# Swapping two entries of a hand-written TensorE order: head 2's transposes ahead of head 3's scores

## The chip, the cores and the metric

The kernel runs on one core of a Trainium2 chip. The core has five engines with instruction streams of their own: TensorE (PE; its weight loads are shown apart as PEld), VectorE (DVE), ScalarE (ACT), GpSimd (POOL) and SyncE (SP, which here issues transfers). TensorE writes its results into PSUM, eight banks of 128 x 512 float32; VectorE and ScalarE move them from there into the on-chip memory SBUF. The metric is device time in microseconds (us), the median of several runs. Lower is better.

## The reference: what is computed

One layer of a causal decoder for 512 tokens of width 1024, in float32: a mixing sublayer (stick-breaking attention with 8 heads beside a short gated convolution), a cross-attention into 256 fixed memory tokens with 4 heads of width 256, a SwiGLU FFN with 2816 hidden channels, and a final RMS norm. The change touches the memory sublayer only:

```
q = (h @ w_q).reshape(b, s, MEM_HEADS, MEM_HEAD_DIM)
kv = (m @ w_kv).reshape(b, mlen, 2, MEM_HEADS, MEM_HEAD_DIM)
scores = jnp.einsum('bshd,bmhd->bhsm', q, k)
probs = jax.nn.softmax(scores / math.sqrt(MEM_HEAD_DIM), axis=-1)
o = jnp.einsum('bhsm,bmhd->bshd', probs, v)
x = x + o.reshape(b, s, D_MODEL) @ w_o
```

(casts to float32 and the RMS norms of `x` and `mem` are left out here).

## The kernel before, in words

Every float32 operand is split into a high and a low part of the type float32r (names that end in `h` and `l`): ScalarE casts the high part, VectorE subtracts it from the original to get the low part. A product is then three matmuls, high x high, high x low and low x high. This is `mm3` (L158 to L161), and `split` (L169) makes the pairs. Weights come through `load_w` (L143): a transfer on SP's queue, a cast `wh` (L154), a subtraction `wl` (L155).

The kernel goes through the sublayers one after another: projections and mixing, the merge, the output projection, the queries of the memory attention, the memory attention, the FFN, the final norm.

In the memory attention the work of a head h, numbered 0 to 3, is cut into parts:

- `mem_q(h)` splits the queries, on ScalarE and VectorE alone. `mem_k(m)` makes 128 rows of keys; a head has two.
- `mem_scores(h)` (L828): 24 matmuls of 256 columns into two PSUM tiles `sc`, then the softmax, still unturned: maxima `mx` (VectorE, L844), the scaled negative `nb` (L847), four exponentials with their sums (ScalarE, L854), a reciprocal `rsu` (L858), and four scalings of the weights `pr` (VectorE, L860).
- `mem_turn(h)` (L865): eight 128 x 128 transposes of `pr` on TensorE into two PSUM tiles `pt`, and their split into `pth` (ScalarE, L173) and `ptl` (VectorE, L174).
- `mem_v(n)` (L811): the values of two heads at once, 96 matmuls of 512 columns, split into `vmh` and `vml` (L176, L177). Heads 2 and 3 need `mem_v(1)`.
- `mem_out(h)` (L873): twice six matmuls of 512 columns (values by turned weights), each six into a PSUM tile `om` that is split into `omh` and `oml`.
- `last(m, k0, k1)` is the output projection's block m, k steps k0 to k1 (function `block`, L617). Two k steps belong to each head: 0 to 5 need the outputs of heads 0 to 2, steps 6 and 7 that of head 3. Its PSUM tile is called `r`.

TensorE's order is written by hand: a list of parts (L885 to L892) stands inside `tc.manual_schedule(engines={mybir.EngineType.PE})`, so TensorE executes its instructions in the order in which the list calls the parts. ScalarE's and VectorE's order in this stage is left to a planner, which runs when the kernel is built: it simulates the engines and takes, for each, among the instructions that it believes ready the one that stands first in the code. On the chip each engine then runs its own instructions in the planned order, and waits where an input is not there.

The tiles come from pools with a fixed number of buffers: `sc` and most `om` from the pool `z` (4 PSUM banks), `pt` and head 1's `om` from the pool `o` (2 banks), `vm` and the projection's first blocks from the pool `mm` (2 banks), split results from a pool of 50 SBUF units, `pr` from a pool of 7.

Of the kernel before, what the change touches and what calls it, by code (L numbers as in the profile page):

```python
# [44 lines left out]
def hybrid_layer(ctx: ExitStack, tc: tile.TileContext, xT_d, memT_d, cols_d, wv_d, win_d,  # L45
# [838 lines left out]
    with tc.manual_schedule(engines={mybir.EngineType.PE}):  # L884
        for part, *args in ((mem_q, 0), (mem_k, 0), (mem_k, 1), (mem_scale,), (mem_k, 2), (mem_k, 3),  # L885
                            (mem_q, 1), (mem_scores, 0), (mem_k, 4), (mem_k, 5), (mem_scores, 1),
                            (mem_q, 2), (mem_k, 6), (mem_k, 7), (mem_turn, 0), (mem_v, 0),
                            (mem_turn, 1), (mem_scores, 2), (mem_q, 3), (mem_out, 0), (mem_out, 1),
                            (mem_v, 1), (mem_scores, 3), (mem_turn, 2), (mem_out, 2),
                            (last, 0, 0, 6), (last, 1, 0, 2), (mem_turn, 3), (last, 1, 2, 6),  # L890
                            (mem_out, 3), (last, 2, 0, 6, otile), (last, 0, 6, 8), (last, 1, 6, 8),
                            (last, 2, 6, 8)):  # L892
            part(*args)
        for m in range(3, KD):
            last(m, 0, KD)
# [305 lines left out]
```

## Time and profile before

| | us |
|---|---|
| three runs | 857.15, 858.88, 859.0 (median 858.88) |
| profiled execution | 856.19 |
| its span, first to last instruction | 854.5 |
| TensorE busy | 843.9 |
| VectorE busy | 644.7 |
| ScalarE busy | 460.6 |

The granted TensorE clock was 0.999 of full speed. Of 114.71 MB moved, 110.65 MB were read from device memory, 132 GB/s over the span. The memory attention's stage, from the first scores to the end of head 3's output, lies between 398.4 and 469.6 us of the span.

In the rows of the profile, `L870 PE MATMUL pt<-ident,pr` means line 870, TensorE, a matmul into the tile `pt` from `ident` and `pr`. In a timeline the first column is the start in us from the span's start, the second the duration, `x8` the number of instructions merged in a row, and the brackets at the end give how long the engine sat idle before and what released it. In a list of waits the columns are us in total, times, and the longest.

### The profile page before, as it was taken

The numbers are of one execution on the slowest core, as the hardware profiler recorded it, in microseconds if no ns is written. First come the engines' busy times: TensorE is split into PE (matmuls) and PEld (weight loads), VectorE is DVE, ScalarE is ACT, GpSimd is POOL, SyncE is SP. The second block draws the span as 40 slices with busy tenths as digits, with TensorE's granted clock in tenths as the row PEclk, the third lists the DMA queues.
The fourth block names the chain that finished last, engine by engine and source line by source line (L and its number), as shares of the span: only waits on it lengthen the run. The fifth ranks groups of instructions, "written<-read, shape, count | busy, mean of one in ns | idle before, by whom it ended". The sixth has DMA issues, their size and how long they took to land.

```text
span 854.5 us, 13535 instructions
## 1 busy us (share of the span) xinstructions
PE 843.9 (99%) x5200; PEld 757.8 (89%) x5200; DVE 644.7 (75%) x1106; ACT 460.6 (54%) x822; POOL 76.9 (9%) x101
## 2 busy tenths in 40 slices
PE   9999999999999999999998999999999999999997
PEld 7888787888888888999987889999999999888997
DVE  8769889986454467878764789888888778876864
ACT  7556766664333345666563666555544556652444
POOL 1011112211000001000000110111111110010002
PEclk9999999999999999999999999999999999999999
DMA  8432232218323343664431428777677775462312
GB/s 297 130 117 82 92 106 81 86 50 276 111 94 99 99 119 91 181 200 151 147 102 49 128 57 198 187 182 186 174 180 188 190 189 168 130 148 65 104 37 100
DMA packets 47217, 114.71 MB, mean 134 GB/s; under 512 B 4912, under 2 KB 9008, under 8 KB 47152
## 3 DMA queue, kind: packets, MB, share of 16 engines
q1 hardware_dynamic: 38704, 97.82, 34.9%
q0 software_dynamic: 8160, 15.73, 11.5%
q8 instruction: 41, 0.67, 0.3%
q10 hardware_dynamic: 288, 0.29, 0.1%
q14 instruction: 24, 0.20, 0.1%
HBM read 110.65 MB, written 2.10 MB: 132 GB/s over the span
## 4 chain that ended last, share of the span: by engine, by line
PE 98%; DVE 1%; ACT 0%; issue 0%; POOL 0%; DVEq 0%; ACTq 0%; POOLq 0%
PE z L710 20%; PE y L710 10%; PE pr L159 8%; PE pr L160 8%; PE pr L161 8%; PE v L710 5%; PE r L159 3%; PE r L160 3%; PE r L161 3%; PE f L160 3%; PE f L159 3%; PE f L161 3%; PE v L265 3%; PE br L160 2%; PE br L159 2%; PE br L161 2%
## 5 line engine op out<-in xcount | busy, mean ns | idle before, releaser
L154 ACT CAST wh<-wr 128x1024 fp32r<-128x1024 f32 x90 | 94.2, 1050 | 131.5 <-issue 48.4
L155 DVE TENSOR_TENSOR wl<-wr,wh 128x1024 fp32r<-128x1024 f32 x90 | 109.7, 1222 | 18.0 <-ACT wh L154 17.4
L159 PE MATMUL pr<-xgh,wh 128*128 128x512 f32 x288 | 112.6, 391 | 0.0
L160 PE MATMUL pr<-xgl,wh 128*128 128x512 f32 x288 | 112.3, 390 | 0.0
L161 PE MATMUL pr<-xgh,wl 128*128 128x512 f32 x288 | 112.2, 390 | 0.0
L710 PE MATMUL z<-xdh,wf 128*128 128x256 f32 x480 | 95.7, 283 | 0.0
L710 PEld LDWEIGHTS z<-xdh,wf 128*128 128x128 f32 x480 | 78.9, 192 | 0.0
L710 PE MATMUL z<-xdl,wf 128*128 128x256 f32 x240 | 67.9, 283 | 0.0
L733 ACT COPY sa<-z 128x256 f32<-128x256 f32 x52 | 19.4, 373 | 85.5 <-PE z L710 85.5
L161 PEld LDWEIGHTS pr<-xgh,wl 128*128 128x128 f32 x288 | 54.1, 188 | 11.4
L159 PEld LDWEIGHTS pr<-xgh,wh 128*128 128x128 f32 x288 | 54.1, 188 | 11.2 <-DVE rv L128 0.3
L160 PEld LDWEIGHTS pr<-xgl,wh 128*128 128x128 f32 x288 | 54.1, 188 | 10.7
L701 DVE TENSOR_TENSOR wf<-s,wf 128x512 fp32r<-128x512 f32 x60 | 41.3, 690 | 22.7 <-ACT wf L700 21.5
L667 POOL DMA_DIRECT2D ws<-in_w_ffn_in_dram x22 | 26.5, 1202 | 305.3 <-DMA ws<-in_w_ffn_in_dram 147.3
L700 ACT CAST wf<-ws 128x512 fp32r<-128x512 f32 x60 | 36.9, 618 | 25.0 <-PE r L160 10.1
L160 PE MATMUL f<-actl,wh 128*128 128x512 f32 (+1 forms) x144 | 49.3, 342 | 0.0
L159 PE MATMUL f<-acth,wh 128*128 128x512 f32 (+1 forms) x144 | 49.3, 342 | 0.0
L161 PE MATMUL f<-acth,wl 128*128 128x512 f32 (+1 forms) x144 | 49.1, 342 | 0.0
L692 DVE TENSOR_TENSOR wf<-wg,wf 128x1024 fp32r<-128x1024 f32 x30 | 36.7, 1224 | 16.1 <-ACT wf L691 16.0
L710 PE MATMUL y<-xch,wf 128*128 128x256 f32 x240 | 48.5, 283 | 0.0
L710 PE MATMUL v<-xoh,wf 128*128 128x256 f32 x240 | 48.5, 283 | 0.0
L710 PE MATMUL z<-xf,wf 128*128 128x256 f32 x360 | 48.4, 283 | 0.0
(295 smaller groups left out, 2296.6 us busy)
## 6 DMA issues: line engine op xcount, KB each, us to landing
wr<-in_w_in_dram SPq DMA_DIRECT2D x36, 512.0 KB, 3.5
ws<-in_w_ffn_in_dram SPq DMA_DIRECT2D x22, 512.0 KB, 4.0
ws<-in_w_ffn_in_dram POOLq DMA_DIRECT2D x22, 512.0 KB, 5.8
wg<-in_w_ffn_in_dram SPq DMA_DIRECT2D x22, 512.0 KB, 4.6
wr<-in_w_ffn_out_dram SPq DMA_DIRECT2D x14, 512.0 KB, 3.5
a<-in_w_ffn_in_dram SPq DMA_DIRECT2D x22, 256.0 KB, 4.8
wr<-in_w_branch_dram SPq DMA_DIRECT2D x8, 512.0 KB, 3.5
wr<-in_w_mix_out_dram SPq DMA_DIRECT2D x8, 512.0 KB, 3.5
```

The costliest lines, as they stand in the source:

```text
L154: after(nc.scalar.copy(h2, raw), lead[-1:])
L155: lows.append(nc.vector.tensor_tensor(out=l2, in0=raw, in1=f(h2), op=ALU.subtract))
L159: nc.tensor.matmul(ps, a[0], b[0], start=start, stop=False, **kw)
L160: nc.tensor.matmul(ps, a[0], b[1], start=False, stop=False, **kw)
L161: nc.tensor.matmul(ps, a[1], b[0], start=False, stop=stop, **kw)
L265: nc.tensor.matmul(vps[t], xg[k][a][:, sl], wv[k][b], start=k == 0 and (a, b) == (0, 0), stop=k == KD - 1 and a == 1)
L667: nc.gpsimd.dma_start(s13, a[:, 0:4:3, :], accum_op=ALU.add)
L692: nc.vector.tensor_tensor(out=lo, in0=pair, in1=f(hi), op=ALU.subtract)
L700: nc.scalar.copy(hi, raw)
L701: nc.vector.tensor_tensor(out=lo, in0=raw, in1=f(hi), op=ALU.subtract)
L710: nc.tensor.matmul(ps[:, :HS], a, b, start=i < 3 and k == 0 and j == 0, stop=k == KP - 1 and j == 2, skip_group_check=True)
L733: nc.scalar.copy((s[:, :HS], None, None, s[:, HS:], t[:, :HS], t[:, :HS])[i], z)
```

## The change

Two neighbours of TensorE's list change places. Before, head 3's scores are written, then head 2's turn and head 2's output; after, head 2's turn is written first, then head 3's scores, then head 2's output. (The parts are numbered from 0: `mem_turn, 2` is the third head's turn, `mem_scores, 3` the fourth head's scores.)

```
-                            (mem_v, 1), (mem_scores, 3), (mem_turn, 2), (mem_out, 2),
+                            (mem_v, 1), (mem_turn, 2), (mem_scores, 3), (mem_out, 2),
                             (last, 0, 0, 6), (last, 1, 0, 2), (mem_turn, 3), (last, 1, 2, 6),
                             (mem_out, 3), (last, 2, 0, 6, otile), (last, 0, 6, 8), (last, 1, 6, 8),
                             (last, 2, 6, 8)):
```

Since the parts are called in this order, the ScalarE and VectorE instructions of head 2's turn (two casts `pth`, two subtractions `ptl`) also stand ahead of head 3's softmax in the code that the planner reads. Instructions, sizes, pools and transfers are the same.

More of the change, by code (lines that the diff above doesn't have):

```diff
@@ L888, in hybrid_layer @@
                             (mem_turn, 1), (mem_scores, 2), (mem_q, 3), (mem_out, 0), (mem_out, 1),
-                            (mem_v, 1), (mem_scores, 3), (mem_turn, 2), (mem_out, 2),
+                            (mem_v, 1), (mem_turn, 2), (mem_scores, 3), (mem_out, 2),
                             (last, 0, 0, 6), (last, 1, 0, 2), (mem_turn, 3), (last, 1, 2, 6),
```

## The prediction

> **What bounds the kernel now.** I read the page's busy shares and its chain first, to see whether one engine carries the span.
>
> ```profile
> PE 843.9 (99%) x5200; PEld 757.8 (89%) x5200; DVE 644.7 (75%) x1106; ACT 460.6 (54%) x822; POOL 76.9 (9%) x101
> PE 98%; DVE 1%; ACT 0%; issue 0%; POOL 0%; DVEq 0%; ACTq 0%; POOLq 0%
> ```
>
> TensorE is busy 99% and makes up 98% of the chain. What a change of order can win is therefore bounded by TensorE's waits, so the view of waits for TensorE alone over the whole span comes next (columns: us in total, times, longest).
>
> ```profile
> PE om L159 <- ACT pth L173: 2.5, 1, 2.5
> PE warm L224 <- DVE neg L91: 1.6, 1, 1.6
> PE om L160 <- DVE ptl L174: 0.5, 1, 0.5
> ```
>
> There are three, and two of them lie at the place of the change: head 2's output product `om` waits for the two halves of the transposed weights, `pth` (a ScalarE cast) and `ptl` (a VectorE subtraction). The timeline of TensorE shows the place (start, duration, and in brackets the idle time before):
>
> ```profile
> 447.33 0.39 PE L161 MATMUL vm<-wh,mgl 128*128 128x512 f32 x1
> 447.56 0.28 PE L159 MATMUL sc<-kmh,mqh 128*128 128x256 f32 x1
> ...
> 450.43 1.04 PE L870 MATMUL pt<-ident,pr 128*128 128x128 f32 x8
> 454.01 0.50 PE L159 MATMUL om<-pth,vmh 128*128 128x512 f32 x1 [2.54 <-ACT pth L173]
> 454.98 0.50 PE L160 MATMUL om<-ptl,vmh 128*128 128x512 f32 x1 [0.47 <-DVE ptl L174]
> ...
> 457.62 0.39 PE L159 MATMUL r<-omh,wh 128*128 128x512 f32 x1
> ...
> 460.56 0.39 PE L160 MATMUL r<-oml,wh 128*128 128x512 f32 x1
> ...
> 463.06 1.03 PE L870 MATMUL pt<-ident,pr 128*128 128x128 f32 x8
> ```
>
> The order is: head 3's scores (`sc`, 447.56), head 2's eight transposes (450.43), head 2's output (454.01), then the projection (`r`, 457.62), and at 463.06 head 3's own turn. Head 2's turn reads softmax results that were done by 436.25 (the scaling at 435.63, quoted below), so nothing makes it late but its place. Directly behind it stands the product that needs it. ScalarE and VectorE show why the wait is as long as 2.5 us:
>
> ```profile
> 448.34 1.04 ACT L154 CAST wh<-wr 128x1024 fp32r<-128x1024 f32 x1
> 451.18 0.57 ACT L854 ACTIVATE pr<-sc,nb,r1s 128x256 f32<-128x256 f32 x1 [1.80 <-DVE nb L847]
> ...
> 453.37 1.08 ACT L173 CAST pth<-pt 128x512 fp32r<-128x512 f32 x2
> ```
>
> ```profile
> 449.19 0.69 DVE L844 TENSOR_REDUCE mx<-sc 128x2 f32<-128x512 f32 x1
> 449.80 1.22 DVE L155 TENSOR_TENSOR wl<-wr,wh 128x1024 fp32r<-128x1024 f32 x1
> ...
> 453.71 0.62 DVE L860 TENSOR_SCALAR pr<-pr,rsu 128x256 f32<-128x256 f32 x2
> 454.24 1.28 DVE L174 TENSOR_TENSOR ptl<-pt,pth 128x512 fp32r<-128x512 f32 x2
> ```
>
> The transposes end at 450.43 + 1.04 = 451.47, but the four exponentials of head 3's softmax hold ScalarE from 451.18, and the casts `pth` follow only at 453.37. On VectorE `ptl` stands behind the scaling of head 3's weights. So head 3's whole softmax lies inside head 2's wait.
>
> **What the new order does, step by step.** The diff swaps two entries of the list by which TensorE's instructions are written out. No instruction is added or removed: eight transposes, 24 score matmuls and all the evictions stay. No DMA belongs to either entry, so the queues of SP and POOL are passed by nothing. ScalarE's and VectorE's orders are left to the planner, which goes by code order and readiness; the swap raises `pth` and `ptl` ahead of head 3's softmax in both.
>
> The new order already stands once in this kernel, one head earlier: `mem_v` 0, turn 1, scores 2, output 0. That stage is the price list, since the shapes are the same. TensorE, ScalarE and VectorE there:
>
> ```profile
> 427.46 1.03 PE L870 MATMUL pt<-ident,pr 128*128 128x128 f32 x8
> 428.25 0.36 PE L159 MATMUL sc<-kmh,mqh 128*128 128x256 f32 x1
> ...
> 431.21 0.40 PE L159 MATMUL om<-pth,vmh 128*128 128x512 f32 x1
> 431.44 0.40 PE L160 MATMUL om<-ptl,vmh 128*128 128x512 f32 x1
> ...
> 433.96 0.39 PE L159 MATMUL om<-pth,vmh 128*128 128x512 f32 x1
> ```
>
> ```profile
> 429.19 1.07 ACT L173 CAST pth<-pt 128x512 fp32r<-128x512 f32 x2
> ...
> 433.11 0.57 ACT L854 ACTIVATE pr<-sc,nb,r1s 128x256 f32<-128x256 f32 x1 [1.79 <-DVE nb L847]
> ...
> 435.29 2.18 ACT L173 CAST omh<-om 128x512 fp32r<-128x512 f32 x4
> ```
>
> ```profile
> 429.32 1.23 DVE L155 TENSOR_TENSOR wl<-wr,wh 128x1024 fp32r<-128x1024 f32 x1 [0.18 <-ACT wh L154]
> 430.46 1.28 DVE L174 TENSOR_TENSOR ptl<-pt,pth 128x512 fp32r<-128x512 f32 x2
> 431.66 1.28 DVE L844 TENSOR_REDUCE mx<-sc 128x2 f32<-128x512 f32 x2
> ...
> 435.63 0.62 DVE L860 TENSOR_SCALAR pr<-pr,rsu 128x256 f32<-128x256 f32 x2
> 436.17 2.48 DVE L174 TENSOR_TENSOR oml<-om,omh 128x512 fp32r<-128x512 f32 x4
> ```
>
> *TensorE, from the swap to the projection.* Turn and scores take 431.21 − 427.46 = 3.75 us there, and the twelve matmuls of one head's output 433.96 − 431.21 = 2.75, both without a wait. Together 6.50 us. In the kernel before, the same work lies between 447.56 and 457.62: 10.06 us. The difference is 3.56 us. It exceeds the 2.54 + 0.47 = 3.01 us of the waits because the two matmuls at the waits run 0.50 instead of 0.39, and the transposes' last rows are drawn to their end instead of being overlapped. The new projection starts at 447.56 + 6.50 = 454.06.
>
> *The halves of head 2's weights.* Shifted by 447.56 − 427.46 = 20.10 us, `pth` runs 449.29 to 450.36 and `ptl` 450.56 to 451.84, its first half until 450.56 + 0.68 = 451.24. The output starts at 431.21 + 20.10 = 451.31 and its first use of `ptl` comes at 451.54. A margin of 0.3 us, the same as in the analogue, where neither row shows a wait. I take zero; the other end is below, as a rival.
>
> *Head 3's softmax, now later.* Its last scaling ends, shifted, at 435.63 + 0.62 + 20.10 = 456.35, against 453.71 + 0.62 = 454.33 before. Who waits for it is head 3's turn, 463.06 before and 463.06 − 3.56 = 459.50 after. The margin is 3.1 us: nothing, as long as that cover stands.
>
> *Head 2's output evictions, now behind the softmax.* This is what is late next. `omh` and `oml` of head 2 queue up behind the exponentials and scalings, as `omh` at 435.29 and `oml` at 436.17 do in the analogue. Shifted, `oml` starts at 456.27 and its first one ends some 0.69 us later, at 456.96 (an estimate from the 1.28 for two). The projection needs it at its fifth k step, in the L160 matmul that starts 460.56 − 457.62 = 2.94 us into the projection, so at 457.00. No margin at all; the second `oml` ends at about 457.55 and is wanted at 457.68. The bounds: nothing, if the planner lets one scaling go behind it, up to 0.7 us, one VectorE operation late. I take 0.1, since the shifted rows meet the need and the two `mq` splits that burden the analogue's VectorE are absent here.
>
> *Work behind the projection.* All later loads are set off by buffers that TensorE frees, and the view of waits shows no matmul waiting behind 455 us. So 3.5 us earlier there is 3.5 us earlier at the end. A gain beyond 3.56 is excluded: no other wait stands in this stage.
>
> *Sum.* −3.56 + 0.1 = −3.46. The profiled execution took 856.19 us (span 854.5 and 1.69 around it), so 852.7 for its like. It lies 2.69 us under the median of the runs, 858.88, which spread from 857.15 to 859.0. Against the median: 858.88 − 3.46 = 855.4.
>
> **The rivals.**
>
> *The exponentials keep their lead.* ScalarE takes its work in the order written: at 451.47 the transposes were done and `pth` still started only at 453.37, behind exponentials that had begun at 451.18. Should the planner still write the four exponentials first, everything from the scores on moves by the turn's 428.25 − 427.46 = 0.79 us, the wait stays in front of the output, and the result is +0.8: 859.7, slower by under 0.1%. Against it: in the stage of head 1 the same code order has `pth` at 429.19 and the exponentials at 433.11. [...]
>
> *A VectorE wait takes the old one's place.* If the maxima of head 3's scores go ahead of `ptl`, the second maximum cannot start before the last scores (451.31 + about 0.2), ends 0.64 later at about 452.2, and the first `ptl` at about 452.9 instead of 451.24. The output's L160 matmul, due at 451.54, waits about 1.4. That leaves −2.2: 856.7. For it: in the kernel before, a maximum went ahead of a weight split (449.19 and 449.80). Against it: the analogue writes `ptl` (430.46) first.
>
> *The re-planning costs at the hand-over to the FFN (the slower side).* Any swap makes the planner re-do ScalarE's and VectorE's order up to the FFN, and there the FFN's first products get their operands with no margin (a row of the waits between 440 and 510 us, and two of VectorE's timeline):
>
> ```profile
> PEld y L710 <- DVE xcl L174: 0.2, 1, 0.2
> ```
>
> ```profile
> 509.04 0.69 DVE L174 TENSOR_TENSOR xcl<-c,xch 128x512 fp32r<-128x512 f32 x1
> 509.64 0.69 DVE L174 TENSOR_TENSOR xdl<-c,xdh 128x512 fp32r<-128x512 f32 x1
> ```
>
> Each 128 x 512 operation that is put ahead of these two delays TensorE by 0.60 us, the distance of their starts. The gain is gone at 3.46 / 0.60, so at six such operations; with nine, 5.4 − 3.46 = +1.9: 860.8. For it: the place has no slack. Against it: order there follows from the projection's blocks, which all move by the same amount.
>
> **How the numbers follow.** The forecast (−2.86 to −3.56 by its bounds, so 855.3 to 856.0 against the median) 0.74; the VectorE wait 0.13; the exponentials first 0.06; the hand-over 0.07. A difference of 0.2%, 1.7 us, is about what a measurement of this kernel can tell from no change. The first two are faster by more: 0.87. The exponentials' case is within it: 0.06. The hand-over's is slower: 0.07. For the range the forecast stands at 855.4; the runs' own spread of 1.85 us and the profiled execution's lower value widen it down to 853.2, and the VectorE wait with a little spread takes it up to 857.0.
>
> **What will show it.** Right, if TensorE's list of waits holds only the `warm` one; if the eight transposes start at about 447.6 and the scores at 448.4; if `pth` stands before the exponentials on ScalarE; and if the first projection matmul starts 6.5 us behind the last `vm` one. A row of `om L160 <- DVE ptl` says that the maxima went first; `r L160 <- DVE oml` of up to 0.7 that head 2's evictions are the new edge; `pt <- DVE pr` that head 3's turn caught up with its softmax, which would take a softmax more than 3.1 us later than the analogue's. A forecast that fails with all of these absent fails behind the projection.

## The result, and the profile after

| | before | after |
|---|---|---|
| median of six runs, us | 858.4 | 852.61 |
| lowest and highest | 857.15, 859.2 | 851.98, 853.19 |
| profiled execution | 856.19 | 852.67 |
| its span | 854.5 | 851.0 |

The changed kernel takes 0.9933 of the time before, with a 95% interval of 0.992 to 0.9946. That is 5.8 us less by the medians, where 3.5 us were forecast; 852.61 lies below the range. The two profiled executions, however, differ by 856.19 − 852.67 = 3.52 us, close to the forecast 3.46. So the question is not where a gain was lost but where 2.3 us more came from, which the first profile did not show.

First the stage itself. TensorE's list of waits of the changed kernel over the whole span (us in total, times, longest) has one row left, the one at the start:

```profile
PE warm L224 <- DVE neg L91: 1.6, 1, 1.6
```

Its timeline at the place of the change (start, duration, engine, line, operation):

```profile
447.70 1.03 PE L870 MATMUL pt<-ident,pr 128*128 128x128 f32 x8
448.50 0.36 PE L159 MATMUL sc<-kmh,mqh 128*128 128x256 f32 x1
...
451.45 0.40 PE L159 MATMUL om<-pth,vmh 128*128 128x512 f32 x1
451.69 0.40 PE L160 MATMUL om<-ptl,vmh 128*128 128x512 f32 x1
...
454.20 0.39 PE L159 MATMUL r<-omh,wh 128*128 128x512 f32 x1
...
457.15 0.39 PE L160 MATMUL r<-oml,wh 128*128 128x512 f32 x1
...
459.65 1.04 PE L870 MATMUL pt<-ident,pr 128*128 128x128 f32 x8
```

Head 2's turn, head 3's scores and head 2's output stand back to back: 454.20 − 447.70 = 6.50 us, the forecast to the hundredth. ScalarE and VectorE of the changed kernel over the same stretch:

```profile
449.43 1.07 ACT L173 CAST pth<-pt 128x512 fp32r<-128x512 f32 x2
453.04 0.59 ACT L173 CAST omh<-om 128x512 fp32r<-128x512 f32 x1 [2.54 <-PE om L161]
453.52 0.57 ACT L854 ACTIVATE pr<-sc,nb,r1s 128x256 f32<-128x256 f32 x1
...
455.70 0.60 ACT L173 CAST omh<-om 128x512 fp32r<-128x512 f32 x1
```

```profile
450.70 1.28 DVE L174 TENSOR_TENSOR ptl<-pt,pth 128x512 fp32r<-128x512 f32 x2
451.90 1.28 DVE L844 TENSOR_REDUCE mx<-sc 128x2 f32<-128x512 f32 x2
...
453.66 0.69 DVE L174 TENSOR_TENSOR oml<-om,omh 128x512 fp32r<-128x512 f32 x1 [0.29 <-ACT omh L173]
...
456.06 0.62 DVE L860 TENSOR_SCALAR pr<-pr,rsu 128x256 f32<-128x256 f32 x2
456.59 0.68 DVE L174 TENSOR_TENSOR oml<-om,omh 128x512 fp32r<-128x512 f32 x1
```

`pth` and `ptl` now run under the scores, ahead of head 3's maxima and exponentials. One thing differs from the analogue: the planner put the first `omh` (453.04) ahead of the exponentials instead of behind them, so its `oml` is ready at 454.35, long before the 457.15 at which the projection reads it.

### The profile page after: what moved, and what is told of

Same layout as the page of the kernel before. It is cut to its first block, busy times and chain, and to the rows that moved or that the text cites. A ratio compares the mean times of both kernels' runs of the same rounds, so it can differ in the third digit from the quotient of the medians.

```text
span 851.0 us, 13532 instructions
## 1 busy us (share of the span) xinstructions
PE 843.5 (99%) x5200; PEld 757.9 (89%) x5200; DVE 644.3 (76%) x1106; ACT 460.9 (54%) x822; POOL 77.2 (9%) x101
## 4 chain that ended last, share of the span: by engine, by line
PE 99%; DVE 0%; POOL 0%; issue 0%; DVEq 0%; ACT 0%; POOLq 0%
PE z L710 20%; PE y L710 10%; PE pr L159 8%; PE pr L161 8%; PE pr L160 8%; PE v L710 5%; PE r L159 3%; PE r L161 3%; PE r L160 3%; PE f L160 3%; PE f L161 3%; PE f L159 3%; PE v L265 3%; PE br L159 2%; PE br L161 2%; PE br L160 2%
```

## Experiments: where the other 2.3 us were

Three theories stood against each other. A: the wait costs more than its idle time, it also drags TensorE's clock down, and the first profile happened to show an execution in which it did not. B: the wait itself is longer in other executions. C: something elsewhere differs. For every execution of this part the time, the span and the mean granted clock are known; an instruction-by-instruction profile exists for one execution of each kernel. Code is shown in outline.

### E1 and E2: both kernels again, unchanged

> The kernel before, unchanged, to see where its ordinary executions lose what the profiled one (856.19 us) did not. The change's two profiled spans differ by 3.5 us (854.5 and 851.0), its medians by 5.8 us. Theory A (the wait drags TensorE's clock): the executions stand at 857 to 859 us, and where the profiled execution is an ordinary one, the granted clock in the stage behind the wait (454 to 460 us) is under 1.0 and the twelve output matmuls and the projection's first ones are slower than 0.23 us apart, some 2 us in all. Theory B (the wait itself varies): the wait of the output product for pth is 4 to 5 us instead of 2.5, with the clock at 1.0. Theory C (the extra is elsewhere): the stage from 447 to 458 us is as in the first profile, and some other stage is longer by about 2 us.

> The changed kernel, unchanged, on the same chip as the others. All theories: 852.0 to 853.2 us, 5.8 us under the kernel before; the profiled span stands within 0.6 us of 851. Were the 5.8 us a matter of the chip on which it was timed, the difference here would be nearer 3.5.

The changed kernel measured 852.40 (851.99 to 852.79; ratio 0.9944, interval 0.9929 to 0.9958). That is 5.4 us under the 857.79 of the kernel before on the same chip, so the 5.8 us were not a matter of the chip. In E1 the kernel before gave 857.66 from 855.72 to 858.78, and its profiled execution this time is one of 858.38 us. Its TensorE timeline at the place:

```profile
450.34 1.04 PE L870 MATMUL pt<-ident,pr 128*128 128x128 f32 x8
453.91 0.80 PE L159 MATMUL om<-pth,vmh 128*128 128x512 f32 x1 [2.54 <-ACT pth L173]
454.88 0.79 PE L160 MATMUL om<-ptl,vmh 128*128 128x512 f32 x1 [0.18 <-DVE ptl L174]
455.48 0.63 PE L161 MATMUL om<-pth,vml 128*128 128x512 f32 x1
455.90 0.63 PE L159 MATMUL om<-pth,vmh 128*128 128x512 f32 x1
...
459.32 0.63 PE L161 MATMUL om<-pth,vml 128*128 128x512 f32 x1
459.74 0.60 PE L159 MATMUL r<-omh,wh 128*128 128x512 f32 x1
460.17 0.41 PE L160 MATMUL r<-oml,wh 128*128 128x512 f32 x1
460.42 0.40 PE L161 MATMUL r<-omh,wl 128*128 128x512 f32 x1
```

The wait is 2.54 us as in the first profile, which is against B. But behind it the matmuls start 0.43 us apart, not 0.23, for over 6 us, and then within about one matmul they are back. The view by stretches, from the stage's start to the first projection matmul (length, busy time of the five engines with counts, granted clock, DMA share, GB/s), tells it in one row each. The first profile of before:

```profile
447.56:457.62 10.06, 7.05 (x46) 6.03 (x44) 7.37 (x16) 5.67 (x14) 0.00 (x0) 1.00 0.32 107
```

E1, the same kernel:

```profile
447.47:459.74 12.27, 9.55 (x45) 7.75 (x44) 7.49 (x16) 5.67 (x14) 0.00 (x0) 0.74 0.25 87
```

The changed kernel:

```profile
447.70:454.20 6.50, 6.50 (x45) 6.00 (x44) 5.79 (x10) 3.96 (x9) 0.00 (x0) 1.00 0.52 164
```

The same work takes 6.50, 10.06 or 12.27 us. The last step is the granted clock, 0.74 over the stretch. Of E1's 856.7 − 854.5 = 2.2 us of longer span, 12.27 − 10.06 = 2.21 lie here, which is against C.

The executions of the unchanged kernel before, taken together from three chips (12 of E1 and 82 runs beside the experiments), fall into three groups with nothing between 856.06 and 856.99 or between 858.07 and 858.38 (the gap that sets the first group apart is wide, the second is narrow):

| | executions | median us | mean granted clock |
|---|---|---|---|
| no drop | 21 | 855.87 | 0.999 |
| middle group | 33 | 857.48 | 0.996 to 0.998 |
| slowest group | 40 | 858.82 | 0.994 to 0.996, one 0.998 |

The steps are 1.6 and 1.3 us. The first profile, at 856.19 and with a clock of 1.00 in the stage, had by chance fallen on the rarest kind. Of the two groups with a drop only the slowest has a profile, E1's; the middle one is told by its times and clocks.

### E3: work in the wait

```
 (mem_v, 1), (mem_scores, 3), (mem_turn, 2),
+(filler, 10),
 (mem_out, 2),
 ...
+def filler(n):
+    ps = mmtile("fill")
+    for _ in range(n):
+        nc.tensor.matmul(ps, vm[0][0][0][:, :P], vm[1][0][0], start=True, stop=True)
```

> The kernel before with ten extra 128x512 matmuls (on two value tiles, into a bank nobody reads) between head 2's turn and head 2's output: 10 x 0.227 = 2.3 us of TensorE work inside the 2.5 us wait, so the wait's end does not move. Theory A: the clock no longer drops, time falls by about 2.2 us to 856.2 although work was added. Theories B and C: time stays at 858.4 within 0.3.

Measured 856.29 (855.49 to 856.79), 0.9984 of the kernel before with an interval of 0.9973 to 0.9994: all twelve executions in one group, none with a clock below 0.999. Added work made the kernel faster, by 1.5 us against the 857.79 of the kernel before on the same chip. TensorE's timeline shows that the wait's end stood where it was:

```profile
451.27 2.54 PE L886 MATMUL fill<-vmh,vmh 128*128 128x512 f32 x10
454.06 0.50 PE L159 MATMUL om<-pth,vmh 128*128 128x512 f32 x1 [0.25 <-ACT pth L173]
455.03 0.51 PE L160 MATMUL om<-ptl,vmh 128*128 128x512 f32 x1 [0.47 <-DVE ptl L174]
...
457.65 0.39 PE L159 MATMUL r<-omh,wh 128*128 128x512 f32 x1
```

The projection starts at 457.65, with the output matmuls at their full pace. This is the cleanest separation of the two prices: the wait's own price is still paid, 856.29 − 852.40 = 3.9 us above the changed kernel, and the clock's part is gone. B and C fall.

### E4: a longer wait

```
+src = tmp("slow")
+nc.scalar.copy(src, pt[m])   # three times, for head 2's first tile
-split(pt[m], "pt")
+split(src, "pt")
```

> The kernel before with three extra copies of the first turned tile on ScalarE ahead of its cast (the cast then reads the copy), which lengthens the wait by 3 x 0.54 = 1.6 us. Theory A: more than the 1.6, up to 1.6 + 1.7, because an idle stretch of over 4 us lets the clock drop every time; the spread of the executions gets smaller. Theories B and C: +1.6 within 0.3, so 860.0.

Measured 859.69 (858.54 to 860.5), +1.8 over the 857.85 that is the median of the 94 executions. The wait for `pth` is 4.4 us, so 1.9 longer, and the second wait, for `ptl`, is gone:

```profile
PE om L159 <- ACT pth L173: 4.4, 1, 4.4
```

The 1.7 us that theory A's bound puts on the clock was the author's estimate. No execution was free of the drop: the lowest lies 2.7 above 855.87, more than the 1.9 us of longer wait, and the clock stood at 0.994 to 0.997 in all twelve. The spread shrank as theory A had it, but the median rose by no more than the wait, since most executions of the kernel before had dropped already. The median alone, 859.69, also fits the 860.0 within 0.3 of B and C; it is the clock of all twelve that speaks for A.

### E5 and E6: a shorter wait

E5 is E3 with `(filler, 5)`. E6 keeps the kernel before and writes head 2's evictions with a priority above head 3's softmax:

```
-pts[h] = [split(pt[m], "pt") for m in range(MT)]
+with tc.high_priority(1000 if h == 2 else 0):
+    pts[h] = [split(pt[m], "pt") for m in range(MT)]
```

> The kernel before with five extra matmuls instead of ten in the wait: 1.1 us of work, so that some 1.4 us of idle time stay in front of the output product and the wait's end does not move. If the clock drops only after an idle stretch of more than about 2 us, all executions stand at 855.7 to 856.6 us, like those of the kernel before with a clock of 0.999. If any wait of over 1 us can trigger it, the two groups of the kernel before (856 and 857 to 859) stay, median 857.8.

> The kernel before, its TensorE order kept, with head 2's two casts and two subtractions planned at a higher priority: they stand between head 3's exponentials instead of behind all four. The first wait shrinks from 2.5 to about 1.0 us. Theory A: about 1.2 us saved on the wait and the clock stays up: 854.5 to 855.0, all executions in one group. Without the clock's part: 1.2 us under the kernel before, 856.6. Should head 3's softmax, now later, hold up head 3's turn, a row of TensorE waiting for pr shows it; there were 8 us of cover before, so no.

E5: 856.58 (855.47 to 857.82). Eight of twelve executions stand at or below 856.63, four lie between 857.13 and 857.82 with a clock of 0.997 or 0.998. Neither expectation was right: with idle waits of 1.39 and 0.47 us the drop still came, but less often (4 of 12). The profiled execution, at span 855.4, is one with it:

```profile
453.43 0.50 PE L159 MATMUL om<-pth,vmh 128*128 128x512 f32 x1 [1.39 <-ACT pth L173]
454.40 0.50 PE L160 MATMUL om<-ptl,vmh 128*128 128x512 f32 x1 [0.47 <-DVE ptl L174]
...
454.97 0.40 PE L159 MATMUL om<-pth,vmh 128*128 128x512 f32 x1
455.20 0.51 PE L160 MATMUL om<-ptl,vmh 128*128 128x512 f32 x1
455.51 0.63 PE L161 MATMUL om<-pth,vml 128*128 128x512 f32 x1
...
458.50 0.51 PE L159 MATMUL r<-omh,wh 128*128 128x512 f32 x1
458.85 0.39 PE L160 MATMUL r<-oml,wh 128*128 128x512 f32 x1
```

Here the clock fell when TensorE was at work again, during the matmul of 455.20, and came back during that of 458.50. The granted clock reads 0.50 over just this stretch, 3.41 us, and in E1 over one of twice the length, 6.83 us (views by stretches of E5, then of E1):

```profile
455.33:458.74 3.41, 3.41 (x10) 2.63 (x9) 0.69 (x1) 0.59 (x2) 0.00 (x0) 0.50 0.00 0
```

```profile
453.36:460.19 6.83, 6.10 (x14) 4.43 (x15) 2.67 (x6) 1.78 (x5) 0.00 (x0) 0.50 0.03 11
```

E6: 854.78 (853.96 to 855.27; ratio 0.9967, interval 0.9955 to 0.9978), 3.1 us under the kernel before. The waits shrank to 0.9 and 0.2:

```profile
PE om L159 <- ACT pth L173: 0.9, 1, 0.9
PE om L160 <- DVE ptl L174: 0.2, 1, 0.2
```

From the transposes to the projection its TensorE needs 456.36 − 450.69 = 5.67 us, where the kernel before needs 457.62 − 450.43 = 7.19:

```profile
450.69 1.03 PE L870 MATMUL pt<-ident,pr 128*128 128x128 f32 x8
...
456.36 0.40 PE L159 MATMUL r<-omh,wh 128*128 128x512 f32 x1
```

So in these two traces 1.5 us come from the waits, where 1.2 were expected, and all ten executions lie in one group. By the medians it is less: 854.78 is 1.1 under the 855.87 of the executions without the drop, and by that reckoning the other 2.0 of the 3.1 us are the drop's. The two figures for the waits, 1.5 and 1.1, were not brought together. The order of the evictions alone brings over half of the gain. The swap is better, since it leaves no wait at all.

### E7 and E8: a wait of its own making, at another place of the changed kernel

```
-(last, 0, 0, 6), (last, 1, 0, 2), (mem_turn, 3),
+(last, 0, 0, 6), (pause, n), (last, 1, 0, 2), (mem_turn, 3),
+def pause(n):                       # n = 4 in E7, 2 in E8
+    ps = otile("pa")
+    nc.tensor.matmul(ps, vm[0][0][0][:, :P], vm[1][0][0], start=True, stop=True)
+    t = unit("pause")
+    for _ in range(n):
+        nc.scalar.copy(t, ps)
+    ps = otile("pb")
+    nc.tensor.matmul(ps, t[:, :P], vm[1][0][0], start=True, stop=True)
```

> The changed kernel with a wait of its own making at another place, between the first and the second block of the output projection: one extra matmul, four copies of its result on ScalarE, one extra matmul that reads the copy. TensorE idles 4 x 0.54 + 0.3 = 2.5 us, 2.9 us longer with the two matmuls. If the second price belongs to the wait's length (theory A): 852.5 + 2.9 = 855.4 for the executions in which the clock stays up, 2 to 3 us more for the others, two groups, median near 857.5. If it belongs to the place or to the old order: 855.4, one group.

> The same with two copies: TensorE idles about 1.4 us, 1.8 us longer with the two matmuls. Theory A with a threshold of about 2 us: 854.3, one group, clock 0.999. If any wait lets the clock drop: two groups, 854.3 and 856.5.

TensorE's wait is 2.53 us in E7 and 1.29 in E8:

```profile
460.49 0.50 PE L890 MATMUL pb<-vmh,pause 128*128 128x512 f32 x1 [2.53 <-ACT pause L888]
```

```profile
459.50 0.50 PE L890 MATMUL pb<-vmh,pause 128*128 128x512 f32 x1 [1.29 <-ACT pause L888]
```

E7 gave two groups: nine executions at 855.23 to 855.99 and three at 857.42 to 858.02 with a clock of 0.997. So the second price goes with the wait and not with the place or the old order; but it came in a quarter of the executions, where most were expected. (The three are told by time and clock; the profiled execution is one of the nine.) E8 gave one group, 853.92 to 855.30, none 1.6 us above the rest. Five of its nine, those from 854.69 up, have a mean clock of 0.998. That is no drop by itself: E6's profiled execution has 0.998 too, and there the granted clock is 1.00 up to 848 us and falls only behind TensorE's last matmul (0.70 from 848 to 853 us). But none of E8's five was profiled, so a drop shorter than the others is not excluded in them.

### E9 and E10: does idle time count together?

The kernel before has its second wait, of 0.5 us, one matmul behind the first. E9 adds such a second one to E7 (a short copy of `pb`'s result and a matmul `pc` that reads it). E10 takes the kernel before and fills its second wait:

```
 nc.tensor.matmul(ps, w[0][:, sl], b[0], start=True, stop=False)     # waits for pth
+fill = mmtile("fill")
+for _ in range(3):
+    nc.tensor.matmul(fill, vm[0][0][0][:, :P], vm[1][0][0], start=True, stop=True)
 nc.tensor.matmul(ps, w[0][:, sl], b[1], start=False, stop=False)    # waits for ptl
```

> The changed kernel with the long wait of its own (2.5 us) and, one matmul behind it, a second wait of about 0.6 us (one short copy and a matmul that reads it), as the kernel before has 2.5 and then 0.5 one matmul later. The clock dropped in 3 of 12 executions with the 2.5 us alone, and in some three quarters of those of the kernel before. If the idle time within a stretch of some microseconds counts together, the share here rises to about three quarters: median near 858.5 (855.8 plus 1.0 for the second wait and its matmul, plus 2). If the length of a single wait counts, it stays at a quarter: median 856.8.

> The kernel before with three extra matmuls between the first output matmul, which waits for pth, and the second, which waits for ptl: 3 x 0.227 = 0.68 us of work inside the second wait, whose end does not move; the first wait of 2.5 us stays as it is. If idle time counts together, the executions with a dropped clock fall from three quarters to about a quarter: median 856.0. If the single wait counts, nothing changes: 857.8.

E9: four executions at 856.19 to 856.49, five at 857.64 to 858.10, three at 859.92 to 860.32; median 857.83. Eight of twelve dropped, against three in E7, and the three groups of the kernel before are back; the median lies between the two that were expected, 858.5 and 856.8. Its profiled execution, one of the middle group (span 855.9), again shows the drop behind the waits, with the transposes at half pace (1.91 us instead of 1.04):

```profile
461.35 0.50 PE L894 MATMUL pc<-vmh,pause 128*128 128x512 f32 x1 [0.35 <-ACT pause L892]
...
462.62 0.63 PE L160 MATMUL r<-oml,wh 128*128 128x512 f32 x1
...
463.47 1.91 PE L870 MATMUL pt<-ident,pr 128*128 128x128 f32 x8
...
466.02 0.40 PE L161 MATMUL r<-omh,wl 128*128 128x512 f32 x1
```

E10: 855.91 (855.47 to 858.01), nine executions at or below 856.44 and three from 857.16 on. Its first wait is unchanged and its second filled:

```profile
453.77 0.50 PE L882 MATMUL om<-pth,vmh 128*128 128x512 f32 x1 [2.54 <-ACT pth L173]
454.11 0.88 PE L885 MATMUL fill<-vmh,vmh 128*128 128x512 f32 x3
454.82 0.42 PE L886 MATMUL om<-ptl,vmh 128*128 128x512 f32 x1
```

Three matmuls of no use, in a wait of 0.5 us, took 1.7 us off the 857.62 of the kernel before on the same chip, though neither product started earlier: the `ptl` one comes 454.82 − 450.20 = 4.62 us behind the start of the transposes, against 454.98 − 450.43 = 4.55. The median expected for idle time that counts together was 856.0. With 3 of 12 against 73 of 94 executions dropped, E10 shows that the second wait, 0.5 us one matmul behind the first, counts beside its 2.5 us; E9 against E7 points the same way but would not show it alone. The shares side by side:

| kernel | waits, us | executions with the drop, by time and clock |
|---|---|---|
| E3 | 0.25 and 0.47 | 0 of 12 |
| E6 | 0.9 and 0.2 | 0 of 10 |
| E8 | 1.3 | 0 of 9 |
| E5 | 1.4 and 0.5 | 4 of 12 |
| E7 | 2.5 | 3 of 12 |
| E10 | 2.5 | 3 of 12 |
| E9 | 2.5 and 0.4 | 8 of 12 |
| before | 2.5 and 0.5 | 73 of 94 |
| E4 | 4.4 | 12 of 12 |

With twelve executions each, neighbouring rows are not told apart; the ends are.

## Why the prediction was wrong

**The wait and its removal: right.** Stage length 6.50 us forecast, 6.50 measured; `pth` forecast at 449.29, found at 449.43; `ptl` at 450.56, found at 450.70; the scores at 448.4, found at 448.50; no matmul waits any more. Span against span the gain is 854.5 − 851.0 = 3.5, forecast 3.46.

**The evictions of head 2: the cost was not there.** The estimate put the first `oml` at 456.96, just in time, and set 0.1 us aside. The planner placed that pair ahead of the exponentials and scalings, and it ended at 453.66 + 0.69 = 454.35. The second ended at 456.59 + 0.68 = 457.27, and the projection wanted it 0.68 us after the 457.15 of the first, at 457.83.

**Head 3's softmax: right.** It ended at 456.06 + 0.62 = 456.68, and the turn came at 459.65: 3.0 us of cover, 3.1 forecast.

**The rivals.** None came about. The exponentials did not keep their lead, the maxima stand behind `ptl`, and at the hand-over to the FFN the wait of the weight load for `xcl` is 0.2 us as before.

**The step that failed** is in the paragraph on the work behind the projection: "A gain beyond 3.56 is excluded: no other wait stands in this stage." It took the price of a wait to be its length. In 73 of 94 executions of the kernel before, by their times and clocks, the wait is followed by a stretch at half TensorE clock (6.83 us in E1, part of it still in the wait), which costs 1.61 us in one group and 2.95 in the other; over all executions that is (33 x 1.61 + 40 x 2.95) / 94 = 1.8 us on the mean, and by the medians 857.85 − 855.87 = 2.0. Together with the wait it makes up the gain: 3.5 + 2.0 = 5.5 against 857.85 − 852.40 = 5.45 in the later executions, and 5.8 in the first comparison, whose six executions before held none of the group without the drop. How the 5.4 us split is known to some 0.4 us only: by E3, which keeps the wait and loses the drop in every execution, they are 3.9 and 1.5.

**What could have been read.** The profile showed a clock of 1.00 from 0 to 848 us, so the drop was not in it. Its time was a hint: 856.19 lay 2.69 us under the median and 0.96 under the lowest of the runs, and the prediction subtracted from the median as if this were a shift of no meaning. A profile faster than every run, with a wait of 2.5 us in it, and a spread of 1.85 us in the runs could together have raised the question of a second price that only some executions pay. The spread alone would not have: the changed kernel's six runs spread over 1.2 us without it.

## What to carry to other kernels

In this kernel, waits of TensorE of 1.3 us and less brought no drop that the times show, while 1.4 and 0.5 close together did in a third of the executions and 4.4 in all. So price such a wait, from those 1.9 us on and with its near neighbours counted in, at its length and, by chance, at up to the 2.95 us more that the clock behind it cost here. Where a profiled execution is faster than all timed ones, find out what it escaped before its sum is taken from their median. Moving an independent TensorE part between a product's last transposes and their first reader hid the eviction chain here (3.5 us of span); where no such part exists, filler matmuls in the wait can pay for themselves, as they did in E3 (1.5 us) and E10 (1.7 us).

## What the runs showed of the hardware that was not expected

The granted clock fell to half for 3.41 us in E5 (0.50 from 455.33 to 458.74) and for 6.83 us in E1 (0.50 from 453.36 to 460.19). In E4 it read 0.67 from 453 to 460 and 0.62 from 460 to 463, with 1.00 before and after; at 0.50 that makes 2 x (0.33 x 7.0 + 0.38 x 3.0) = 6.9 us, an estimate. In E9 the pace was halved from 462.62 to 466.02, 3.4 us: the matmuls of 462.62 and of 465.60 were each followed by the next after 0.42 us, those before and behind after 0.23. Nor did the clock fall only while TensorE idled. In E5 the second of the two waits had ended at 454.40, and TensorE had been at work for 0.93 us when the clock fell; in E9 it had ended at 461.35, 1.27 us before the half pace began.

An estimate from these lengths: at a clock of 0.50 the 3.41 us of E5, TensorE busy throughout, cost at most 3.41 / 2 = 1.7 us, and the 6.83 us of E1, with TensorE busy for 6.10 of them, 6.10 / 2 = 3.05. The groups of the kernel before (855.87, 857.48, 858.82) stand 1.61 and 2.95 us above the first, so they fit no such stretch, a short one and a long one, though no execution of the middle group was profiled.

Behind TensorE's last matmul the clock fell as well. In the first profile of before that matmul ends at 848.57, and the clock reads 1.00 up to 852.50, 0.62 from there to 853.00 and 0.50 after. In the changed kernel the last one ends at 845.15, and the clock reads 1.00 up to 849, 0.82 from there to 850 and 0.50 after. So by both traces it fell some 4.0 and 4.5 us after the last matmul (an estimate from the means).

The length of a wait does not decide alone. The 2.54 and 0.47 us of the first profile, the 2.54 of E10's and the 2.53 of E7's were not followed by the drop, while the 2.54 and 0.18 of E1's and the 1.39 and 0.47 of E5's were followed by the drop. Over the executions 2.5 us alone had it in 6 of 24 (E7 and E10), two waits of 1.4 and 0.5 us in 4 of 12. What decides in the single execution was not shown.
